# Weights of a matmul with batch norm: a pair of blocks first, two single blocks behind

## The chip, the cores and the metric

The kernel runs on one core of a Trainium2 chip. The metric is the device time of one execution in microseconds (us), the median of three runs. The core has five engines with their own instruction streams: PE (TensorE, matmuls; its weight loads are listed as PEld), DVE (VectorE), ACT (ScalarE), POOL (GpSimd) and SP (SyncE, which here issues stores and DMA transposes). Sixteen DMA engines move the data.

## The reference

```python
batch, m, k, n = 16, 512, 1024, 768

def reference(x, weight, gamma, beta, eps):
    y = np.matmul(x, weight)
    mean = np.mean(y, axis=(0, 1), keepdims=True)
    var = np.var(y, axis=(0, 1), keepdims=True)
    y_norm = (y - mean) / np.sqrt(var + eps)
    return (gamma * y_norm + beta).astype(np.float32)
```

The rows of all batches form one matrix of 8192 x 1024, multiplied by a 1024 x 768 weight matrix. Each of the 768 columns of the product is normalised over all its 8192 rows. All arrays are float32.

## The kernel before, in words

**Tiles.** The 8192 rows are cut into 16 chunks of 512 (`CH`). The first two chunks are loaded in halves of 256 rows (`QR`), the later ones whole. Every load converts float32 to bf16 on the way, and only POOL issues such loads. A load of x is four issues, one for each quarter of the 1024 elements of k, each into 32 partitions (L386 to L394). DVE then turns the chunk (STREAM_TRANSPOSE, L403 to L422) so that k lies on the partitions; for chunk 0 each half is turned in two pieces, of two blocks of k each. The turned chunk is the tile `xT_sb`.

**Weights.** k is cut into four blocks (`JW` = 4), numbered by `jw`; one block of w covers 256 elements of k, all 768 columns. `load_w(jw, jw1)` (L378) loads the blocks from jw up to jw1, again with four issues, each into 32 partitions. `w_ready` holds the load task by its first block; `waits` (L592) lets a matmul unit wait for all loads of w whose first block is at most its own last block.

**Loads in order.** The list `order` (L426 to L431) writes the order of the loads by hand: `("x", 0)` is the first half of chunk 0, which is called x0 here, then x1 (its second half), x2 and x3 (the halves of chunk 1); `("w", a, b)` is the load of blocks a to b - 1. Before, this is x0, block 0, x1, block 1, blocks 2 and 3 together, x2, x3, then whole chunks.

**Matmuls.** The first 256 columns (two column tiles, `GA`) are computed with rows on the partitions (`rows_unit`, L598, matmuls at L493); the other 512 columns, four column tiles, with columns on the partitions (`col_unit`, L610, matmuls at L558). `part(q0, q1, jws)` (L757) does for the halves q0 up to q1 of chunk 0 all products with the blocks in `jws`. The order before (L763 to L771) is: first half with block 0; a filler; second half with block 0; both halves with block 1; both halves with blocks 2 and 3 together. Then, from L822 on, the later chunks follow: rows, then columns for the first chunks; the other columns are computed after the loads are over.

**Warm-up and filler.** TensorE begins with `WAKE` = 8 matmuls of zeros in float32 (L574; each is two instructions) and `SMALL` = 22 small ones in bf16 (L577). The filler is the same float32 matmul, `FILL` times.

**Statistics.** When a row unit is done, ACT squares it (L642), DVE adds the rows (L645), POOL or DVE adds the squares (L649), and ACT keeps a bf16 copy (L655). When a column unit is done, DVE takes its statistics (L694) and ACT keeps a copy (L698). Eight PSUM banks hold the results until then.

**Planner.** Nothing is issued in the order of the code. Each piece of work becomes a `Task` with a priority (a due time), the engines it can run on, an assumed duration and what it depends on. `arrange` (L122) plays the schedule through with these durations and writes a fixed order of instructions for every engine. `clock[0]` (L580) adds up the assumed durations of TensorE's work and gives the due times of what follows. The class `Wires` assumes eight loads in flight for each queue (`LANES`).

Of the kernel before, what the change touches and what calls it, by code (L numbers as in the profile page):

```python
# [227 lines left out]
def kernel(  # L228
# [20 lines left out]
    NT = N // P  # L249
# [6 lines left out]
    JW = KQ // 64  # L256
    PIECES = ((0,QR),(QR,QR))
    WAKE = 8
    FILL = 2
    SMALL = 22  # L260
    TOUCH = 1
    EARLY = 4
    SHORT = 2
    GA = 2
# [26 lines left out]
    def seq(bi):  # L291

        ins = bi.ins
        prev = last.get(ins.engine)
        if prev is not None:
            tc.add_manual_dep(
                ins, prev,
                mybir.DependencyInfo(mybir.DependencyClass.NoSync, mybir.DependencyReason.DATA),
                reason="order",
            )  # L300
        last[ins.engine] = ins.name
        return bi
# [48 lines left out]
    def task(prio, engines, emit, deps=(), lock=False, **kw):  # L351
        t = Task(prio, engines, emit, deps, **kw)
        t.lock = lock
        tasks.append(t)
        return t

    def dve(occ):
        return {"DVE": (occ, occ + 0.09)}

    def act(occ):  # L360
        return {"ACT": (occ, occ + 0.11)}
# [14 lines left out]
    w_ready, x_ready, x_slot, plain, last_loads = {}, {}, {}, {}, []  # L376

    def load_w(jw, jw1):  # L378
        def emit(eng):
            rows = weight.rearrange("(i jw c e) n -> i c jw (e n)", i=4, jw=JW, e=2)  # L380
            dst = w_sb.rearrange("p jw e n -> p jw (e n)")
            for i in range(4):
                seq(nc.gpsimd.dma_start(dst[32 * i:32 * i + 32, jw:jw1], rows[i, :, jw:jw1]))
        return emit

    def load_x(m0, rows, slot):  # L386
        def emit(eng):
            x_bf = piece(slot).bitcast(bf16).rearrange("p (t k) -> p t k", k=KQ)
            slot.tile = x_bf
            src = x_flat[m0:m0 + rows].rearrange("(t r) k -> r t k", r=32)  # L390
            for i in range(4):
                bi = seq(nc.gpsimd.dma_start(x_bf[32 * i:32 * i + 32], src[:, :, KQ * i:KQ * (i + 1)]))  # L392
            slot.loader.ins = bi.ins
        return emit  # L394
# [28 lines left out]

    for c in range(C):
        x_slot[c] = Slot(xts)
    order = [("x", 0), ("w", 0, 1)] + [("x", 1), ("w", 1, 2), ("w", 2, 4)]  # L426
    order += [("x", q) for q in range(2, SHORT * QPC)] + [("c", c) for c in range(SHORT, C - 1)]
    at = M - CH
    for rows in (CH-P,P):
# [2 lines left out]
    t = 1.0  # L432
    affine = None
    for kind, n, *n1 in order:
        if kind == "w":
            took = 4 * 192 * 4 * (n1[0] - n) / 4 * PER_KB * 1.024
            w_ready[n] = task(t, {"POOL": (2.0, 2.0)}, load_w(n, *n1), dma=took)
            w_ready[n].count = 4
            t += 2.1 * (n1[0] - n)
            if n1[0] == JW:  # L440
                idt = task(t, {"POOL": (0.6, 0.6)}, lambda eng: make_identity(nc, ident))
                task(t, act(0.25), lambda eng: seq(nc.scalar.copy(ident32, ident)), [idt])
            continue
        rows = n1[0] if kind == "p" else QR if kind == "x" else CH
        m0 = n if kind == "p" else n * rows
        if m0 == M // 2:
            affine = task(t, {"SP": (5.0, 7.0)}, load_affine, [x_ready[m0 // CH - 3, 0, JW]])
        slot = Slot(rings, rows // 32 * KQ // 2)
        load = task(
            t, {"POOL": (2.68 * rows / CH, 2.68 * rows / CH)}, load_x(m0, rows, slot), dma=rows * K * 4 / 1024 * PER_KB * 1.024,  # L450
            takes=[slot])
        load.count = 4
        slot.loader = load
        last_loads.append(load)
        t += 2.7 * rows / QR
        for i in range(rows // QR):
            c, q = divmod(m0 // QR + i, QPC)
            for j0, j1 in ((0, JW // 2), (JW // 2, JW)) if m0 < CH else ((0, JW),):
                new = q == 0 and j0 == 0
                x_ready[c, q, j1] = task(  # L460
                    -1000 + t, dve((2.2 if c in SINGLE else 1.16) * (j1 - j0) / JW + 0.02),
                    turn_x(slot, x_slot[c], m0, i * QR // 32, j0, j1, new), [load],
                    uses=[slot] if new else [slot, x_slot[c]], takes=[x_slot[c]] if new else [])
                if not new:
                    x_ready[c, q, j1].deps.append(x_ready[c, 0, JW // 2 if m0 < CH else JW])
            x_ready.setdefault((c, q, JW // 2), x_ready[c, q, JW])
        if rows % QR:
            t0 = rows // QR * QR // 32
            m1 = m0 + 32 * t0
            c, q = divmod(m1 // QR, QPC)  # L470
            x_ready["tile", m1 // P] = task(
                -1000 + t, dve(0.63), turn_x(slot, x_slot[c], m0, t0, 0, JW, False, P),
                [load, x_ready[c, 0, JW]], uses=[slot, x_slot[c]])
            x_ready[c, q, JW] = x_ready[c, q, JW // 2] = x_ready["tile", m1 // P]
# [95 lines left out]
    def wake(count, slot):  # L570
        def emit(eng):
            idle_ps = psum.tile([P, CH], f32, tag="b")
            for _ in range(count):
                seq(nc.tensor.matmul(idle_ps, idle_sb[:, 0:P], idle_sb, start=True, stop=True))  # L574
            small = idle_sb[:, 0:P // 2].bitcast(bf16)
            for _ in range(SMALL if count == WAKE else 0):
                seq(nc.tensor.matmul(idle_ps[:, 0:P], small, small, start=True, stop=True))  # L577
        return emit
# [5 lines left out]
    def pe_task(occ, emit, deps, key=None, **kw):  # L584
        t = task(clock[0], pe(occ), emit, deps, **kw)
        t.after = begun.get(key)
        begun[key] = t if key else None
        emit.task = t
        clock[0] += occ
        return t  # L590

    def waits(jws, c, q0, q1):  # L592
        return [w_ready[w] for w in w_ready if w <= jws[-1]] + [
            x_ready[c, q, JW // 2 if jws[-1] < JW // 2 else JW] for q in range(q0, q1)]
# [3 lines left out]
    def rows_unit(c, ts, jws=range(JW)):  # L598
        key = "row", c, ts[0]
        slot = bank_of.setdefault(key, None) or Slot(banks)  # L600
        bank_of[key] = slot
        kw = {"takes": [slot], "uses": [x_slot[c]]} if jws[0] == 0 else {"uses": [slot, x_slot[c]]}
        h = ts[0] * P // QR
        t = pe_task(0.873 * len(ts) * len(jws) / JW, mm_rows(c, ts, list(jws), slot),
                    waits(jws, c, h, h + 1), key, **kw)
        if jws[-1] == JW - 1:
            rows_stats(c, ts, slot, t)
        return t

    def col_unit(nt, c, jws, q0=0, q1=QPC):  # L610
        slot = bank_of.setdefault((nt, c), None) or Slot(banks)
        bank_of[nt, c] = slot
        first = jws[0] == 0 and q0 == 0
        xs = [plain[c][0][jw] for jw in jws] if c in plain else [x_slot[c]]
        kw = {"takes": [slot], "uses": xs} if first else {"uses": [slot] + xs}
        t = pe_task((1.728 if c in plain or c in SINGLE else 1.808) * len(jws) / JW * (q1 - q0) / QPC,
                    mm(nt, c, list(jws), slot, q0, q1),
                    waits(jws, c, q0, q1) + ([plain[c][1][jw] for jw in jws] if c in plain else []), (nt, c), **kw)
        if q1 - q0 == QPC:
            t.hosts = 4  # L620
        if jws[-1] == JW - 1 and q1 == QPC:
            col_stats(nt, c, slot, t)
        return t
# [133 lines left out]
    def part(q0, q1, jws):  # L757
        for h in range(q0, q1):
            rows_unit(0, [2 * h, 2 * h + 1], jws)
        for nt in range(GA, NT):  # L760
            col_unit(nt, 0, jws, q0, q1)

    part(0, 1, [0])  # L763
    fill_slot = Slot(banks)
    pe_task(0.87 * FILL, wake(FILL, fill_slot), [w_ready[0]], takes=[fill_slot])
    part(1, 2, [0])
    part(0, 2, [1])
    for h in range(2):
        rows_unit(0, [2 * h, 2 * h + 1], [2, 3])
    for nt in range(GA, NT):  # L770
        col_unit(nt, 0, [2, 3])  # L771

    halves = [range(JW // 2), range(JW // 2, JW)]
    merges = []
# [455 lines left out]
    nt = NT - 1  # L1230
# [40 lines left out]
    for c, r0, rows in ends:  # L1271
        due = E + 2.0 + 0.6 * c
        n = max(rows // CH, 1)
# [30 lines left out]
    order = arrange(tasks, turns)  # L1304
# [39 lines left out]
```

## Time and profile before

| what | value |
|---|---|
| runs | 208.77, 208.78, 208.35 us; median 208.77 |
| span of the profiled execution | 206.5 us |
| loads of x by POOL: issues of 256 KB | 52, median 8.8 us from issue to landing |
| loads of w by POOL: issues of 96 KB (one block) | 8, median 5.1 us to landing |
| loads of w by POOL: issues of 192 KB (two blocks) | 4, median 5.9 us to landing |
| turns of x0 and x1 on DVE, each in two pieces | begin at 8.49 and 13.45 us, 1.31 and 1.30 us |
| turns of x2 and x3 on DVE | begin at 22.65 and 25.71 us |
| four issues of x0 on POOL | from 1.29 us, 2.44 us |
| four issues of block 0 of w on POOL | from 3.73 us, 1.99 us |
| one issue of x1 on POOL | 5.84 us, and the next at 6.76 us |

The span is the time from the first to the last record of one profiled execution; the measured time of a run is longer, since it holds what lies around the span. A KB in the sizes is counted as the data is written to SBUF, in bf16. L12 is line 12 of the kernel. The granted clock is the share of TensorE's full clock that it was given. A line of the timeline merges neighbouring instructions of one kind; its length is that of the group, so neighbouring groups of matmuls, which are pipelined, overlap a little.

### The profile page before, as it was taken

Reading aid. Unit: us, or ns where it says so; the run is one execution under the profiler, and the core shown is the slowest. Engines: PE = TensorE matmul, PEld = TensorE weight load, DVE = VectorE, ACT = ScalarE, POOL = GpSimd, SP = SyncE. Lnnn points to the kernel's source line nnn. Section 1 sums busy time; section 2 is a strip of 40 time slices with the busy share of each in tenths; the row PEclk is TensorE's granted clock in tenths of the full one; section 3 lists DMA queues with packets and bytes.
Section 4 is the critical chain, followed back from the end, with each engine's and each line's share of the span. In section 5 each row is a group of like instructions: output and inputs, shape, how many; then the busy total and the mean of one; then the engine's idle time right before and its main releaser. Section 6 shows DMA issues by size and latency. Waiting matters only on the chain.

```text
span 206.5 us, 3506 instructions
## 1 busy us (share of the span) xinstructions
PE 191.4 (93%) x1211; PEld 116.3 (56%) x1226; DVE 156.3 (76%) x238; ACT 139.8 (68%) x248; POOL 132.0 (64%) x148
## 2 busy tenths in 40 slices
PE   7998999999999999999999999999999999996900
PEld 3465564747488888777875444444444445553600
DVE  4220779999999999968989998977999648947900
ACT  2000560369989999998978767997376776866950
POOL 7877964877488999999304999599954440440000
PEclk9999999999999999999999999999999999999995
DMA  5999999999999999999676898999999999999898
GB/s 55 169 168 193 192 196 196 196 198 197 190 193 197 197 197 195 196 197 195 110 120 199 311 339 307 267 350 307 315 317 245 291 325 308 274 341 347 254 347 243
DMA packets 98497, 48.73 MB, mean 236 GB/s; under 512 B 24240, under 2 KB 97968, under 8 KB 98480
## 3 DMA queue, kind: packets, MB, share of 16 engines
q0 software_dynamic: 34688, 18.36, 65.1%
q1 hardware_dynamic: 63792, 30.16, 52.8%
q8 instruction: 9, 0.15, 0.3%
q14 instruction: 8, 0.07, 0.1%
HBM read 36.71 MB, written 25.17 MB: 300 GB/s over the span
## 4 chain that ended last, share of the span: by engine, by line
PE 82%; DMA 8%; ACT 3%; issue 1%; POOL 1%; DVE 1%; ACTq 0%; POOLq 0%
PE y_ps L558 51%; PE y_ps L493 23%; DMA ring<-in_x_dram 5%; PE y_ps L798 4%; ACT o_sb L1293 3%; DMA w_sb<-in_weight_dram 3%; PE o_ps L1028 2%; PE a_ps L887 1%; POOL ring L392 1%; PE y_ps L736 1%; PE o_ps L1058 0%; ACTq L1339 0%; PE tot_ps L855 0%; DVE fin L743 0%; ACT y_sb L746 0%
## 5 line engine op out<-in xcount | busy, mean ns | idle before, releaser
L558 PEld LDWEIGHTS <-w_sb 128*128 128x128 bf16 x512 | 49.7, 97 | 57.4
L558 PE MATMUL y_ps<-x_pl,w_sb 128*128 128x512 bf16 x256 | 60.5, 379 | 0.3
L392 POOL DMA_DIRECT2D ring<-in_x_dram x76 | 47.5, 630 | 13.0 <-DVE xT_sb L414 5.0
L558 PE MATMUL y_ps<-xT_sb,w_sb 128*128 128x512 bf16 (+1 forms) x241 | 55.1, 376 | 0.4
L493 PE MATMUL y_ps<-w_sb,xT_sb 128*128 128x256 bf16 x448 | 50.7, 273 | 0.6 <-DMA w_sb<-in_weight_dram 0.6
L493 PEld LDWEIGHTS <-xT_sb 128*128 128x128 bf16 x448 | 43.6, 98 | 8.3 <-issue 1.7
L421 DVE STREAM_TRANSPOSE xT_sb<-ring 128x1024 f32<-128x1024 f32 (+1 forms) x29 | 31.2, 1111 | 12.4 <-DMA ring<-in_x_dram 12.2
L694 DVE BATCH_NORM_STATS2 stats<-y_ps 128x6 f32<-128x512 f32 x46 | 30.9, 687 | 12.7 <-PE y_ps L558 12.5
L698 ACT CAST y_sb<-y_ps 128x512 bf16<-128x512 f32 x51 | 29.4, 590 | 14.5 <-DVE stats L694 12.4
L926 POOL TENSOR_TENSOR ring<-ring,sum 128x1024 f32<-128x1024 f32 (+1 forms) x11 | 23.7, 2193 | 14.6 <-DVE ring L921 14.5
L649 POOL TENSOR_TENSOR sum<-sum,sq_sb 128x512 f32<-128x512 f32 x21 | 26.9, 1281 | 3.2 <-ACT sq_sb L642 2.1
L642 ACT ACTIVATE sq_sb<-y_ps 128x512 f32<-128x512 f32 x28 | 16.3, 607 | 18.0 <-PE y_ps L493 17.1
L645 DVE TENSOR_TENSOR sum<-y_ps,sum 128x512 f32<-128x512 f32 x28 | 18.9, 675 | 9.1 <-ACT sq_sb L642 7.8
L530 ACT COPY x_pl<-xT_sb 128x1024 bf16<-128x1024 bf16 x24 | 24.4, 1052 | 1.7 <-DVE xT_sb L421 1.7
L655 ACT CAST y_sb<-y_ps 128x512 bf16<-128x512 f32 x28 | 16.0, 599 | 7.8 <-DVE sum L645 7.6
L530 POOL COPY x_pl<-xT_sb 128x1024 bf16<-128x1024 bf16 x15 | 16.1, 1108 | 8.0 <-DVE x_pl L530 5.2
L921 DVE TENSOR_TENSOR ring<-y_sb,a_ps 128x1024 f32<-128x1024 bf16 (+1 forms) x16 | 16.7, 1080 | 0.3 <-DMA out_dram<-ring 0.3
L1139 POOL TENSOR_TENSOR ring<-ring,sum 128x1024 f32<-128x1024 f32 x4 | 9.6, 2412 | 11.0 <-DVE ring L1135 11.0
L1193 ACT CAST ring<-ring 128x1024 f32<-128x1024 bf16 x15 | 15.7, 1049 | 1.0 <-DMA ring<-y_sb 1.0
L1028 PE MATMUL o_ps<-ident,y_sb 128*128 128x128 bf16 x104 | 14.2, 221 | 2.2 <-DVE y_sb L1280 2.0
L414 DVE STREAM_TRANSPOSE xT_sb<-ring 128x2048 bf16<-128x2048 bf16 x6 | 13.5, 2289 | 0.2 <-DMA ring<-in_x_dram 0.2
L574 PE MATMUL idle_ps<-idle_sb 128*128 128x512 f32 x20 | 11.2, 717 | 1.5 <-DVE idle_sb L314 1.5
(97 smaller groups left out, 155.0 us busy)
## 6 DMA issues: line engine op xcount, KB each, us to landing
out_dram<-ring SPq DMA_DIRECT2D x38, 512.0 KB, 3.7
ring<-in_x_dram POOLq DMA_DIRECT2D x52, 256.0 KB, 8.8
out_dram<-o_sb SPq DMA_DIRECT2D x6, 512.0 KB, 4.9
ring<-in_x_dram POOLq DMA_DIRECT2D x16, 128.0 KB, 5.3
out_dram<-ring SPq DMA_DIRECT2D x4, 256.0 KB, 3.0
w_sb<-in_weight_dram POOLq DMA_DIRECT2D x8, 96.0 KB, 5.1
w_sb<-in_weight_dram POOLq DMA_DIRECT2D x4, 192.0 KB, 5.9
ring<-in_x_dram POOLq DMA_DIRECT2D x4, 192.0 KB, 8.1
```

The lines of the kernel that those rows point to most:

```text
L392: bi = seq(nc.gpsimd.dma_start(x_bf[32 * i:32 * i + 32], src[:, :, KQ * i:KQ * (i + 1)]))
L421: seq(nc.vector.transpose(dst, src[:, :, jw0:jw1]))
L493: seq(nc.tensor.matmul(y_ps[:, s], x_of(c, jw, e, t * P, (t + 1) * P), w_sb[:, jw, e, 0:NA], start=(s == 0 and jw == 0 and e == 0), stop=( ...
L530: seq(nc.scalar.copy(dst, pairs) if eng == "ACT" else ENG[eng].tensor_copy(dst, pairs))
L558: seq(nc.tensor.matmul(y_ps, w_sb[:, jw, e, nt * P:(nt + 1) * P], moving(c, jw, e, q0 * QR, q1 * QR, parted), start=(jw == 0 and e == 0 an ...
L645: seq(nc.vector.tensor_add(sum1, slot.tile[:, 0:n], sum1))
L649: seq(ENG[eng].tensor_add(acc, acc, state["sq"][:, 0:n]))
L694: seq(nc.vector.bn_stats(dst, slot.tile))
L698: seq(nc.scalar.copy(y(nt, c), slot.tile))
L921: seq(nc.vector.tensor_mul(slot.o, y_row[c].y[:, s0:s1], aff[0][:, None, :].to_broadcast([P, n, NA])))
L926: seq(ENG[eng].tensor_add(slot.o, slot.o, row[:, None, :].to_broadcast([P, n, NA])))
L1028: seq(nc.tensor.transpose(dst, src, ident))
```

## The change

```diff
-    FILL = 2
-    SMALL = 22
+    FILL = 1
+    SMALL = 34
...
-    order = [("x", 0), ("w", 0, 1)] + [("x", 1), ("w", 1, 2), ("w", 2, 4)]
+    order = [("x", 0), ("w", 0, 2), ("x", 1), ("w", 2, 3), ("w", 3, 4)]
...
-            w_ready[n] = task(t, {"POOL": (2.0, 2.0)}, load_w(n, *n1), dma=took)
+            w_ready[n] = task(t, {"POOL": (2.14, 2.14)}, load_w(n, *n1), dma=took)
...
-    part(0, 1, [0])
+    part(0, 1, [0, 1])
     fill_slot = Slot(banks)
     pe_task(0.87 * FILL, wake(FILL, fill_slot), [w_ready[0]], takes=[fill_slot])
-    part(1, 2, [0])
-    part(0, 2, [1])
-    for h in range(2):
-        rows_unit(0, [2 * h, 2 * h + 1], [2, 3])
-    for nt in range(GA, NT):
-        col_unit(nt, 0, [2, 3])
+    part(1, 2, [0, 1])
+    part(0, 2, [2])
+    part(0, 2, [3])
```

The loads become: x0, blocks 0 and 1 of w together, x1, block 2, block 3, x2, x3. TensorE does the first half of chunk 0 with blocks 0 and 1 (half of k), one filler matmul, the second half with blocks 0 and 1, then both halves with block 2 (a quarter of k), and both halves with block 3. Twelve more small matmuls stand at the end of the warm-up. The planner assumes 2.14 us of POOL's time for a load of w instead of 2.0. The number of issues stays: four double and eight single ones for w.

## The prediction

> **What bounds the kernel now.** I read the page's busy times and the chain that ended last, then the waits of TensorE, then the first 30 us engine by engine, then the bytes moved in each 2 us. The page first.
>
> ```profile
> span 206.5 us, 3506 instructions
> PE 191.4 (93%) x1211; PEld 116.3 (56%) x1226; DVE 156.3 (76%) x238; ACT 139.8 (68%) x248; POOL 132.0 (64%) x148
> PE 82%; DMA 8%; ACT 3%; issue 1%; POOL 1%; DVE 1%; ACTq 0%; POOLq 0%
> ```
>
> TensorE bounds it: 82% of the chain. The waits of TensorE, whole list (total, times, longest):
>
> ```profile
> PE o_ps L1028 <- DVE y_sb L1280: 2.0, 1, 2.0
> PE idle_ps L574 <- DVE idle_sb L314: 1.5, 1, 1.5
> PE y_ps L493 <- DMA w_sb<-in_weight_dram: 0.6, 1, 0.6
> ```
>
> One is at the start, one at the very end (190.9 us), and one, 0.6 us, in chunk 0. From 20 to 189 us TensorE waits for nothing listed, so what TensorE gains or loses before 29 us should reach the end one for one. The places that matter, from the timeline (start, length, engine, line, what; in brackets the idle time before and what ended it):
>
> ```profile
> 10.67 1.39 PE L577 MATMUL idle_ps<-idle_sb 128*128 128x128 bf16 x22
> 11.89 0.60 PE L493 MATMUL y_ps<-w_sb,xT_sb 128*128 128x256 bf16 x4
> 13.24 1.88 PE L574 MATMUL idle_ps<-idle_sb 128*128 128x512 f32 x4
> 19.74 1.91 PE L493 MATMUL y_ps<-w_sb,xT_sb 128*128 128x256 bf16 x16 [0.60 <-DMA w_sb<-in_weight_dram]
> 25.10 3.83 PE L493 MATMUL y_ps<-w_sb,xT_sb 128*128 128x256 bf16 x32
> 25.71 1.25 DVE L421 STREAM_TRANSPOSE xT_sb<-ring 128x1024 f32<-128x1024 f32 x1 [0.64 <-DMA ring<-in_x_dram]
> 27.01 1.64 PEld L493 LDWEIGHTS <-xT_sb 128*128 128x128 bf16 x16 [0.28 <-DVE xT_sb L421]
> ```
>
> Chunk 0 runs from 11.89 to 25.10. The first half of chunk 1 follows at 25.10, and its second half at 27.01 is loaded into TensorE only when VectorE has turned it: it lands at about 25.6, is turned from 25.71 to 26.96, and TensorE's weight load waits 0.28 us for it. So **a second limit lies right under the first**: even if chunk 0 ended much earlier, TensorE would stand before this half until 26.96. The stretches of 2 us (busy us of each engine, then granted clock, DMA share, GB/s):
>
> ```profile
> 2.00:4.00 2.00, 2.00 (x3) 0.66 (x2) 1.04 (x4) 0.22 (x2) 2.00 (x5) 1.00 0.60 63
> 4.00:6.00 2.00, 2.00 (x4) 0.74 (x3) 0.00 (x0) 0.00 (x0) 2.00 (x6) 1.00 1.15 130
> 6.00:8.00 2.00, 2.00 (x6) 0.90 (x5) 0.00 (x0) 0.30 (x1) 1.34 (x4) 1.00 1.14 166
> 8.00:10.00 2.00, 2.00 (x6) 0.95 (x5) 1.31 (x2) 0.00 (x0) 1.86 (x4) 1.00 1.19 188
> 10.00:12.00 2.00, 2.00 (x25) 1.42 (x24) 0.00 (x0) 0.00 (x0) 1.86 (x5) 1.00 1.35 177
> 12.00:14.00 2.00, 2.00 (x16) 1.46 (x13) 0.55 (x1) 0.00 (x0) 1.35 (x3) 1.00 1.07 157
> 14.00:16.00 2.00, 2.00 (x13) 1.20 (x12) 0.75 (x2) 0.00 (x0) 1.46 (x4) 1.00 1.04 177
> 16.00:18.00 2.00, 1.94 (x16) 1.42 (x15) 0.00 (x0) 0.00 (x0) 1.56 (x4) 1.00 1.08 207
> 18.00:20.00 2.00, 1.40 (x9) 0.55 (x7) 0.00 (x0) 0.00 (x0) 1.25 (x3) 1.00 1.28 182
> ```
>
> The clock is 1.00 throughout. Adding GB/s x 2 us gives the bytes moved: 0.39 MB by 6 us, 0.72 by 8, 1.09 by 10, 1.45 by 12, 1.76 by 14, 2.12 by 16, 2.53 by 18, 2.89 by 20; the next stretches read 193 and 197, so 3.28 by 22 and 3.67 by 24. The loads are 0.524 MB for a half chunk of x and 0.393 MB for a block of w as written to SBUF. In order, x0+w0+x1 are 1.44 MB, reached at 12.0 us; its last issue lands at about 13.32. All of w is 2.62 MB, reached at 18.5; it lands at about 19.6. x3 (chunk 1's second half) ends at 3.67 MB, reached at 24.0; it lands at 25.6. So **a load lands 1.1 to 1.7 us after its bytes are through; I use 1.35**. GpSimd issues every load itself, and its waits show that the ninth load waits for the first to land (5.84 us, after x0's first, issued at 1.29 and landing 4.5 us later), the next for the second, and so on: eight are in flight.
>
> **The change, part by part.** The sum is made on the profiled execution (span 206.5 us); the runs' median is 208.77, so 2.3 us lie outside the span, which I leave as they are.
>
> *Warm-up, 22 to 34 small matmuls.* They go from 10.67 to 11.89, 0.0555 us each; 12 more are 0.67 us and end at 12.56.
>
> *First w as a pair.* The four issues start at 3.73 as before; the four double ones of before took 0.54 each against 0.50, so GpSimd ends 0.1 us later, before the lane wait at 5.84 that paces x1: no cost. x0 and the pair are 1.31 MB, reached at 11.2, landing at 12.57. Bounds: 11.3 (last issue 5.34, and the doubles of before landed 5.9 us after issue) and 12.9 (lag 1.7). Up to 12.56 the warm-up covers it. I take 12.6, 0.7 us later than 11.89.
>
> *Chunk 0.* A half of one block is 1.35 us (11.89 to 13.24), a whole one 2.7 (two of them from 19.74 to 25.10 are 5.4). The first half of the pair is 2.70: 12.6 to 15.3. The filler falls from two calls to one; two took 1.72 (13.24 to 14.96), so 0.86: to 16.2. x1 ends at 1.835 MB, reached at 14.4, lands at 15.8, and VectorE's first piece (0.65, half of the 1.30 at 13.45) is done at 16.5. TensorE waits 0.3 us there. Second half: 16.5 to 19.2. Block 2 lands at 17.9 (2.23 MB at 16.5) and block 3 at 19.6 to 19.9: both are there in time, so the 0.6 us wait goes. Block 2 runs to 21.9, block 3 to 24.6. Chunk 0 ends **0.5 us earlier** than 25.10. Block 1 is now done in halves, 16 column matmuls of 256 for 8 of 512: 1.82 us (8 took 0.91, from 12.33 to 13.24) against 1.73, and the 0.09 is within the 2.70. Banks: six for chunk 0, two for chunk 1's rows, as before.
>
> *Statistics of chunk 0.* The row sums become due at 22.4 instead of 20.8, and the four column sums (0.68 each on VectorE) come within 2 us instead of 4. VectorE has 3.3 us from 22.4 to 25.7 for one turn of x (1.24) and three row operations (0.69, 0.68, 0.65): it just fits, at nothing, as long as no column sum is put before the turn of x3.
>
> *Loads behind.* The number of issues is unchanged, but eight in flight now hold less: singles stand where the doubles stood, just ahead of x2 and x3. By "landing of the eighth before, plus 0.25" and 0.6 us per x issue: block 2 is issued at 9.6, 10.7, 11.7, 12.8; block 3 at 13.6, 14.4, 15.2, 16.0; x2 from 16.6 (before 14.67); x3's last at **20.75 against 19.89**. In between the transfers in hand (issued over 1.3 us ago and not yet moved) shrink to about 0.2 MB from 17 to 21 us; in the run before they were that few near 12 us, where the row reads 157 GB/s. What x3 loses has two ends: nothing, if bytes set its landing (25.6 as before), and 0.86 us, if its last issue again takes 5.7 us to land, which is what x issues of 17 to 20 us took. x1's issues with as little in hand took 4.7 to 4.8, so neither end is excluded; I take the middle, **0.43 us late**.
>
> A rule of the Trainium skill stands on the other side. "DMA: Bandwidth & Descriptors", section "Anatomy of one DMA — SWDGE (gpsimd) path", fits a GpSimd load as about 2.0 us plus its bytes over 436 GB/s. For x3's last issue that is an estimate of some 2.6 us, landing at 23.4: TensorE would then never wait for it, and the sum would be 0.5 us faster, 208.3. The trace disagrees for such loads (5.7 us), because others are ahead in the queue.
>
> *Sum.* TensorE reaches chunk 1 at 24.6, ends its first half (1.75) at 26.4, and waits for x3: 26.96 + 0.43 = 27.4, against 27.01. The 0.5 us won in chunk 0 is lost in that wait, and **0.4 us is added: 209.2**. Behind it wait chunk 1's columns, and for them chunk 2's rows at 36.0; those need VectorE's turns of 31.09 to 35.59, 0.4 us of slack. They move along with the statistics.
>
> **Rivals.** *The other side, not slower:* the pair puts more in flight early, so the dip at 12 to 14 us (157 against about 190 around it: 0.066 MB, 0.35 us) is filled and no new one opens. x3 then lands 0.35 early, TensorE starts its second half at 26.6, and the time is 208.4, at best 208.2, where chunk 0's end decides (26.4). It decides as soon as x3 lands before 25.6. For: chunk 0's shorter end is sure. Against: 0.86 us of later issue.
>
> *Bytes alone set the landing:* second half at 26.96, no idle elsewhere, 208.7. For: 195 GB/s without gaps from 20 us on. Against: the thin queue before.
>
> *VectorE becomes the bound:* the planner's list puts one more sum (0.68) ahead of the turn of x3, which cannot give way. Then 27.4 + 0.5 to 0.68: 209.7 to 209.9. For: VectorE's 3.3 us fill the gap exactly, and the planner's due times move by 0.87 with the shorter filler, so that its whole list is made anew. Against: in the run before it waited 0.64 us idle for x3.
>
> **How the numbers follow.** Late x3: 0.43, own range 208.8 to 209.7 (0 to 0.86 late), a little over half of it slower by more than 0.2% (0.42 us, about what a measurement of this kernel tells from no change). VectorE: 0.20, slower. Bytes alone: 0.12, no change. More in flight: 0.25, of which 0.18 is beyond the bound. Faster 0.18; same 0.07 + 0.12 + 0.19 = 0.38; slower 0.24 + 0.20 = 0.44. The range, 208.2 to 210.1, goes from the best end of the faster case to VectorE's worst with a queue lag 0.2 more.
>
> **What would show it.** Right: TensorE's first real matmul near 12.6; no wait for w in chunk 0; a wait of 0.5 to 1 us of the row matmuls for the turn of x3 near 27; x3's last issue near 20.7; the remaining chain shifted as a whole. Wrong: x3 turned before 26.9; new waits between 30 and 189 us; a first matmul later than 13.2, which would move every step of chunk 0.

## The result, and the profile after

The changed kernel takes 210.4 us (median of five runs, 210.31 to 210.92) against 208.4 us of the kernel before in the same series; the ratio is 1.0115, with a 95% interval of 1.0091 to 1.014. That is slower by 2.0 us between the medians and by 2.4 us by the ratio, and the median lies 0.3 us beyond the upper end of the predicted range. The profiled execution has a span of 208.9 us, 2.4 more than the 206.5 before. Medians and ratios differ by some tenths of a us in the runs below too; where it matters, both are given.

The page of the changed kernel begins so:

```profile
span 208.9 us, 3557 instructions
PE 192.0 (92%) x1244; PEld 118.6 (57%) x1244; DVE 155.4 (74%) x237; ACT 140.0 (67%) x248; POOL 133.4 (64%) x149
...
PE 53%; POOL 14%; DMA 13%; DVE 6%; issue 6%; ACT 3%; ACTq 0%; DVEq 0%; POOLq 0%
```

TensorE is still the busiest engine, but it is only 53% of the chain that ended last, where it was 82% before; loads of x and their issues on GpSimd (DMA and POOL) have taken its place there. TensorE also holds more instructions: 12 more small warm-up matmuls, 8 more column matmuls (16 of 256 columns for 8 of 512) and 2 fewer in the filler make 18, and as many weight loads (1244 for 1226), so 36 instructions. Its waits, all of them:

```profile
PE o_ps L1025 <- DVE y_sb L1277: 2.0, 1, 2.0
PE idle_ps L574 <- DVE idle_sb L314: 1.5, 1, 1.5
PE y_ps L493 <- DVE xT_sb L421: 1.1, 2, 0.9
PE y_ps L493 <- ACT y_sb L698: 0.3, 1, 0.3
PE y_ps L493 <- DMA w_sb<-in_weight_dram: 0.3, 1, 0.3
```

The 0.6 us wait for w inside chunk 0 is gone; the 0.3 us left stands ahead of the first matmul. In its place are two waits for turned x (0.9 us at 25.7 us, 0.2 at 81.5) and one for ScalarE at 46.2. The timeline of TensorE and VectorE where chunk 0 ends (lines are three lower than before behind the change):

```profile
12.23 1.03 PE L493 MATMUL y_ps<-w_sb,xT_sb 128*128 128x256 bf16 x8 [0.26 <-DMA w_sb<-in_weight_dram]
23.82 1.91 PE L493 MATMUL y_ps<-w_sb,xT_sb 128*128 128x256 bf16 x16
25.32 1.25 DVE L421 STREAM_TRANSPOSE xT_sb<-ring 128x1024 f32<-128x1024 f32 x1
26.63 1.92 PE L493 MATMUL y_ps<-w_sb,xT_sb 128*128 128x256 bf16 x16 [0.90 <-DVE xT_sb L421]
```

Chunk 0 ends 1.3 us earlier (23.82 against 25.10), and chunk 1's second half begins 0.38 us earlier (26.63 against 27.01). So in this execution the start was won, and the loss lies behind it. Two stretches hold it. Chunk 3's rows begin 0.09 us later than before (46.49 against 46.40), the columns that follow the long row stretch 0.49 later (85.23 against 84.74), and TensorE's last long group 0.66 later (185.81 against 185.15): 1.04 us are lost between 27 and 106 us. And from there to the end of the span another 1.7 us are lost, though all the lists of work there are the same. The DMA rate from 195 to 209 us, in 40 slices of 0.35 us, first of the kernel before, then of the changed one, each with the queue lines that differ:

```profile
GB/s 340 345 348 351 344 348 347 345 348 348 345 350 347 342 348 351 345 340 348 351 348 351 340 345 348 351 344 348 193 7 0 0 0 0 0 23 0 0 0 0
...
q14 instruction: 1, 0.01, 0.2%
```

```profile
GB/s 344 345 174 332 388 328 328 318 332 335 345 302 350 347 350 344 345 348 350 347 342 347 350 348 344 347 347 348 348 344 350 70 20 22 22 22 3 0 0 0
...
q8 instruction: 1, 0.02, 0.6%
```

Before, the stores end all at once (the lone 23 behind them is the 8 KB transfer on q14). After, the rate drops to 174 once, at 195.7 to 196.1, and at the end some 22 GB/s go on alone for 1.7 us. 348 over 16 is 21.8: that is **one DMA engine of sixteen, 1.7 us behind the others**. On queue q8, which carries only such transfers, stands one transfer of 16 KB of instructions that the kernel before does not have there. In the trace's packets it begins at 196.63 us; the last store has landed on fifteen engines by 206.36 and on the sixteenth at 208.01. Over the whole run the kernel before has nine such transfers, the last at 179.5 us, and the changed one ten.

So the 2.4 us between the two profiles are 0.66 us of TensorE's lag, 1.48 us of the late engine (1.75 us behind the median engine, where it was 0.27) and 0.25 us more in the stores of the other engines: these land 0.68 us later than before at 196.2 us and 0.85 to 0.91 later from 197.9 on, behind the slice at 174 GB/s. What made that slice is not known.

### The profile page after: what moved, and what is told of

Its sections match the earlier page's. It is cut to its first block, busy times and chain, and to the rows that moved or that the text cites. A ratio compares the mean times of both kernels' runs of the same rounds, so it can differ in the third digit from the quotient of the medians.

```text
span 208.9 us, 3557 instructions
## 1 busy us (share of the span) xinstructions
PE 192.0 (92%) x1244; PEld 118.6 (57%) x1244; DVE 155.4 (74%) x237; ACT 140.0 (67%) x248; POOL 133.4 (64%) x149
## 4 chain that ended last, share of the span: by engine, by line
PE 53%; POOL 14%; DMA 13%; DVE 6%; issue 6%; ACT 3%; ACTq 0%; DVEq 0%; POOLq 0%
PE y_ps L558 39%; DMA ring<-in_x_dram 10%; POOL ring L392 9%; PE y_ps L493 5%; PE y_ps L795 3%; DMA w_sb<-in_weight_dram 3%; POOL sum L649 3%; ACT o_sb L1290 2%; PE o_ps L1025 2%; DVE xT_sb L421 2%; POOL w_sb L383 2%; DVE xT_sb L414 1%; DVE stats L694 1%; PE a_ps L884 1%; PE y_ps L736 1%
## 5 line engine op out<-in xcount | busy, mean ns | idle before, releaser
L558 PEld LDWEIGHTS <-w_sb 128*128 128x128 bf16 x520 | 50.5, 97 | 56.6
L558 PE MATMUL y_ps<-x_pl,w_sb 128*128 128x512 bf16 x264 | 61.3, 379 | 0.0
L558 PE MATMUL y_ps<-xT_sb,w_sb 128*128 128x512 bf16 (+1 forms) x256 | 55.9, 370 | 0.0
L649 POOL TENSOR_TENSOR sum<-sum,sq_sb 128x512 f32<-128x512 f32 x22 | 28.2, 1281 | 2.7 <-ACT sq_sb L642 2.0
L574 PE MATMUL idle_ps<-idle_sb 128*128 128x512 f32 x18 | 9.6, 686 | 1.5 <-DVE idle_sb L314 1.5
```

What stands on the lines that cost most here:

```text
L558: seq(nc.tensor.matmul(y_ps, w_sb[:, jw, e, nt * P:(nt + 1) * P], moving(c, jw, e, q0 * QR, q1 * QR, parted), start=(jw == 0 and e == 0 an ...
L649: seq(ENG[eng].tensor_add(acc, acc, state["sq"][:, 0:n]))
```

## The experiments

Theory F: the tenth instruction transfer delays one DMA engine and so the end. Theory L: the planner's new list, the order of work that it makes for every engine, costs TensorE the 1.04 us. When L fell, theory Q took its place (single blocks behind the pair let the queue of loads run thin), against P (the pieces of chunk 0 or the pair in front).

**a_small18: fewer TensorE instructions in the changed kernel**

```diff
-    SMALL = 34
+    SMALL = 18
```

> The changed kernel with 18 small warm-up matmuls instead of 34: 32 TensorE instructions fewer, nothing else. Theory F (code fetch): in the profile of the changed kernel a tenth 16 KB instruction transfer begins at 196.6 us, when TensorE has 19 instructions left, and from then on one of the 16 DMA engines ends every store 1.75 us after the others; the kernel before has nine such transfers, the last at 179.5 us. With 32 instructions fewer the tenth is not reached: the last store ends on all engines within 0.4 us and the time falls by 1.3 to 1.6 us, from 210.4 to 208.9. The shorter warm-up ends 0.9 us earlier but the first pair of w lands at 12.2 us as before, so nothing is lost there. Rival L (the planner's list alone costs the 2 us): no change, 210.4.

Measured: 209.27 us, ratio to the kernel before 1.0046 (1.0028 to 1.0065), against 1.0115 of the changed kernel. By the ratios 1.4 us of the 2.4 are gone, as F expected; by the medians 1.1, and the median stands 0.4 us above the expected one. There are nine instruction transfers, and the same view of the end:

```profile
GB/s 345 348 341 347 348 350 345 347 347 347 347 347 350 347 347 342 350 348 350 340 347 350 350 342 347 347 348 350 345 347 170 0 0 0 0 0 0 23 0 0
```

No engine is left behind. What remains is TensorE's own lag, 0.68 us at its last long group (185.83). Here x3's half is turned from 26.00, and chunk 1's second half begins at 27.30, 0.29 late:

```profile
24.07 1.92 PE L493 MATMUL y_ps<-w_sb,xT_sb 128*128 128x256 bf16 x16
27.30 0.94 PE L493 MATMUL y_ps<-w_sb,xT_sb 128*128 128x256 bf16 x7 [1.31 <-DVE xT_sb L421]
```

**b_more_pe: more TensorE instructions in the kernel before**

```diff
-    WAKE = 8
+    WAKE = 6
-    SMALL = 22
+    SMALL = 53
```

> The kernel before with two float32 warm-up matmuls fewer and 31 small ones more: the warm-up takes as long as before (1.72 us out, 1.72 us in), the planner's lists of all other engines are the same, and TensorE has some 54 instructions more. Theory F: a tenth 16 KB instruction transfer falls into the last stores, one DMA engine ends about 1.7 us late, and the time rises by 1.3 to 1.7 us, from 208.4 to about 209.9. Rival L: no change, 208.4.

Measured: 209.51 us, ratio 1.0074 (1.0046 to 1.0102): slower by 1.5 us by the ratio, by 1.1 between the medians. TensorE stands where it stood (185.05 against 185.15), and the end has the lone engine again, with the tenth transfer at 196.94 us:

```profile
GB/s 340 344 335 342 347 380 326 323 334 339 350 345 347 344 348 350 350 337 350 350 348 342 348 345 350 350 345 345 107 22 20 22 18 0 0 0 0 0 0 23
...
q8 instruction: 1, 0.02, 0.4%
```

Taken away from one kernel and put into the other, the transfer carries 1.4 and 1.5 us by the ratios, 1.1 both times by the medians. Among all nine profiles of this case the last store has a late engine (by 1.49 to 1.75 us) in just the three with a tenth transfer, and none by more than 0.27 in the six others (table below). F is shown. The Trainium skill ("Runtime: NRT & Kernel Launch", section "Instruction fetch mechanics") says that an engine's code is refilled in blocks of 16 KiB, 256 instructions, and that crossing a boundary is mostly hidden. The blocks agree with the trace: each transfer has 16 KB, and one comes every 248 to 256 TensorE records on average (176 to 322 between two of them). That the cost is hidden holds for the ninth: in the kernel before, the store of 181 us ended on one engine 1.84 us after the median, and this lag was down to 0.25 us by 195.8, after the gap between the stores at 192 us. The tenth came with no gap behind it. No run here singles out what the first eight cost.

**a_listB and b_listA: the planner's lists exchanged**

```diff
-    order = arrange(tasks, turns)
+    order = follow(tasks, turns)
```

Here `follow` takes a fixed list of task, engine and time, that which the planner made for the other kernel; the tasks of both correspond one to one.

> The changed kernel (its loads, its pieces of chunk 0, its warm-up), but every engine follows the list that the planner made for the kernel before, task by task. Theory L in part (the list costs what TensorE loses between 27 and 106 us: it was 0.38 us ahead at chunk 1's second half and 0.66 us behind at 185 us, 1.04 us in all): TensorE stays ahead, and the time falls by about 1.0 us, from 210.4 to 209.4; the tenth instruction transfer stays, as the number of instructions does. Rival (the loss between 27 and 106 us comes from when the loads land, not from the list): within 0.3 us of 210.4.

> The kernel before (its loads, its pieces of chunk 0, its warm-up), but every engine follows the list that the planner made for the changed kernel. Theory L in part: TensorE loses about 1.0 us between 30 and 106 us, and the time rises from 208.4 to 209.4, with no late DMA engine at the end. Rival (loads, not the list): within 0.3 us of 208.4.

Measured: b_listA 208.35 us, ratio 1.0004 (0.9986 to 1.0022); a_listB 212.26 us, ratio 1.0178 (1.014 to 1.0217). The kernel before loses nothing with the changed kernel's list, and the changed kernel gains nothing from the old list but loses 1.3 us more by the ratios, 1.9 by the medians. **Theory L fell.** Why the old list hurts the changed kernel can be read from VectorE's timeline of a_listB:

```profile
22.51 0.69 DVE L645 TENSOR_TENSOR sum<-y_ps,sum 128x512 f32<-128x512 f32 x1 [6.17 <-ACT sq_sb L642]
23.11 2.43 DVE L649 TENSOR_TENSOR sum<-sum,sq_sb 128x512 f32<-128x512 f32 x1
25.46 1.23 DVE L421 STREAM_TRANSPOSE xT_sb<-ring 128x1024 f32<-128x1024 f32 x1
```

It puts a row sum and a sum of squares of chunk 0 ahead of the turn of x2, and these now come later: x2 is turned at 25.46 instead of 22.14, and TensorE waits 2.7 us. The new list turns x2 first. Not all of the 2.7 us is the order, though: the sum of squares took 2.43 us here, where the usual one takes 0.68, for a reason that no run shows.

What the three profiles with the changed loads so far have in common is the loads themselves. The stretches of 2 us of the changed kernel (last number: GB/s):

```profile
14.00:16.00 2.00, 2.00 (x15) 1.24 (x13) 1.06 (x2) 0.00 (x0) 1.60 (x4) 1.00 1.10 206
16.00:18.00 2.00, 2.00 (x20) 1.74 (x18) 0.25 (x1) 0.00 (x0) 2.00 (x5) 1.00 1.12 192
18.00:20.00 2.00, 2.00 (x17) 1.45 (x15) 0.00 (x0) 0.00 (x0) 2.00 (x4) 1.00 1.20 117
20.00:22.00 2.00, 2.00 (x14) 1.25 (x13) 0.00 (x0) 0.22 (x1) 1.81 (x4) 1.00 1.41 184
22.00:24.00 2.00, 2.00 (x12) 0.93 (x11) 1.82 (x2) 0.87 (x3) 1.97 (x3) 1.00 1.29 169
24.00:26.00 2.00, 1.73 (x16) 1.31 (x14) 1.93 (x3) 1.77 (x4) 2.00 (x4) 1.00 1.27 162
```

Up to 16 us the pair is ahead: 2.30 MB of loads have moved, against 2.12 before. Then the rate falls to 117 from 18 to 20 us (182 before), again to 169 and 162 from 22 to 26 (197 and 187 before), and by 28 us 4.32 MB have moved, against 4.43. From there on the loads run at 195 GB/s without a break until about 95 us, so the 0.1 MB, 0.5 us, is not made up: 14.41 against 14.51 MB at 80 us.

**b_singles: the kernel before with blocks 2 and 3 singly**

```diff
-    order = [("x", 0), ("w", 0, 1)] + [("x", 1), ("w", 1, 2), ("w", 2, 4)]
+    order = [("x", 0), ("w", 0, 1)] + [("x", 1), ("w", 1, 2), ("w", 2, 3), ("w", 3, 4)]
```

> The kernel before with blocks 2 and 3 of w loaded one after the other instead of together; the lists of TensorE, VectorE, ScalarE and SyncE are the same, GpSimd has four load issues more. Theory Q (thin queue): eight issues are in flight at most, and with single blocks in them the queue ahead of x2 and x3 runs dry; in the three profiles with single blocks there, the loads moved 89 to 125 GB/s in the stretch from 18 to 19 us and 1.27 to 1.34 MB from 16 to 24 us, in the three with a double block 161 to 181 GB/s and 1.48 to 1.54 MB. The same hole must open here, x is turned late, TensorE waits some 0.5 to 1 us near 27 us and the time rises by 0.5 to 1.0 us, to about 209.1. Rival P (the pieces of chunk 0 or the pair in front cause the loss): no change, 208.4.

Measured: 210.03 us against 207.95, ratio 1.0081 (1.0053 to 1.0109). The loss is larger than expected, 1.7 us by the ratio and 2.1 between the medians, and the eleven runs lie wide apart, 208.69 to 211.27. The profile is of a run of 209.15 and shows only the smaller loss; what the runs of 210 us and more lose besides is not known. No piece of chunk 0 and no entry in the lists of TensorE, VectorE, ScalarE and SyncE has changed, and the hole opens (view as above):

```profile
16.00:18.00 2.00, 2.00 (x17) 1.47 (x16) 0.00 (x0) 0.00 (x0) 1.83 (x4) 1.00 0.98 171
18.00:20.00 2.00, 1.71 (x10) 0.75 (x9) 0.00 (x0) 0.00 (x0) 1.57 (x4) 1.00 0.90 112
20.00:22.00 2.00, 2.00 (x17) 1.50 (x16) 0.68 (x2) 1.03 (x2) 1.31 (x3) 1.00 1.43 190
```

TensorE waits 0.39 us near 27 us, less than expected, and 0.44 again at 81.7. The profile puts this second wait to a square on ScalarE, but the weight load at the same place waits 0.72 us for turned x, and VectorE, which had waited 1.31 us for x until 64.9, has worked almost without a pause since. At its last long group TensorE is 0.88 us behind (186.03). So the second wait at 81 us, where x just keeps pace with the row matmuls, collects what the loads lost at 18 us. A code transfer is not what makes the hole: TensorE's first falls at 17.6 us in the changed kernel, but at 23.7 here, behind the hole.

**b_loadsA: the kernel before with the changed kernel's loads**

```diff
-    order = [("x", 0), ("w", 0, 1)] + [("x", 1), ("w", 1, 2), ("w", 2, 4)]
+    order = [("x", 0), ("w", 0, 2), ("x", 1), ("w", 2, 3), ("w", 3, 4)]
...
-            w_ready[n] = task(t, {"POOL": (2.0, 2.0)}, load_w(n, *n1), dma=took)
+            w_ready[n] = task(t, {"POOL": (2.14, 2.14)}, load_w(n, *n1), dma=took)
```

> The kernel before with the loads of the changed kernel (pair first, then x1 and two single blocks), but its own pieces of chunk 0, its own warm-up and so its own number of TensorE instructions. Theory Q: the hole at 18 us opens, about 0.2 MB less by 24 us, TensorE is 0.5 to 0.7 us behind at 185 us, no tenth instruction transfer, 209.0. Rival P (the pieces): within 0.3 us of 208.4.

Measured: 209.29 us, ratio 1.006 (1.0038 to 1.0081), 1.3 us slower where 0.6 had been expected. 3.54 MB have moved by 24 us against 3.66 before; TensorE waits 1.34 us for x3's half at 26.6, and is 0.93 behind at its last long group (186.08). All of the 0.93 is lost at x3 here, and there is no second wait at 81 us. There are nine instruction transfers and no lone engine. The planner made a new list for this run too (TensorE's pieces stand in another order than before), but a new list alone cost nothing in b_listA, and b_singles has the loss with the lists unchanged. So the loads make this part of the loss, and not the four more issues of b_singles either, since this run has as many as the kernel before; P fell.

**a_two_pairs: the changed kernel with both pairs whole**

```diff
-    SMALL = 34
+    SMALL = 18
...
-    order = [("x", 0), ("w", 0, 2), ("x", 1), ("w", 2, 3), ("w", 3, 4)]
+    order = [("x", 0), ("w", 0, 2), ("x", 1), ("w", 2, 4)]
...
-    part(0, 2, [2])
-    part(0, 2, [3])
+    for h in range(2):
+        rows_unit(0, [2 * h, 2 * h + 1], [2, 3])
+    for nt in range(GA, NT):
+        col_unit(nt, 0, [2, 3])
```

> The changed kernel with blocks 2 and 3 loaded together behind x1 and multiplied together (half and half of k), and 18 small warm-up matmuls. Theory Q with theory F: no hole at 18 us, no tenth instruction transfer, so both losses go and TensorE keeps what it wins in chunk 0: 0.3 to 0.5 us faster than the kernel before, 208.0, and 1.2 us faster than the run with 18 small matmuls alone. Rival P: no better than that run, 209.3.

Measured: 207.65 us against 207.95, ratio 0.998 (0.9962 to 0.9998): a little faster than the kernel before, the fastest here. The stretch of the hole, and TensorE's first real matmul:

```profile
16.00:18.00 2.00, 2.00 (x16) 1.44 (x15) 0.92 (x2) 0.00 (x0) 1.33 (x3) 1.00 1.09 202
18.00:20.00 2.00, 1.93 (x18) 1.46 (x16) 0.00 (x0) 0.00 (x0) 1.22 (x3) 1.00 1.42 192
20.00:22.00 2.00, 2.00 (x16) 1.38 (x15) 0.92 (x2) 1.27 (x3) 1.88 (x4) 1.00 1.44 193
```

```profile
12.91 1.03 PE L493 MATMUL y_ps<-w_sb,xT_sb 128*128 128x256 bf16 x8 [1.66 <-DMA w_sb<-in_weight_dram]
24.74 3.65 PE L493 MATMUL y_ps<-w_sb,xT_sb 128*128 128x256 bf16 x32
```

The hole is closed, x2's first issue comes at 13.72 us instead of 15.58, and all of chunk 1 follows at 24.74 without a wait. Though TensorE idles 1.66 us before its first matmul, it is 0.54 us ahead at its last long group (184.61 against 185.15). A dip from 22 to 26 us is here too (171 and 178), so that second dip is not the single blocks' doing; the hole from 18 to 20 us is.

All runs side by side (ratio to the kernel before; start of TensorE's last long group; how long after the median of the sixteen engines the last store ends on the last one, in the profile):

| run | ratio | last long group, us | last engine, us |
|---|---|---|---|
| before | 1 | 185.15 | 0.27 |
| changed kernel | 1.0115 | 185.81 | 1.75 |
| a_small18 | 1.0046 | 185.83 | 0.12 |
| b_more_pe | 1.0074 | 185.05 | 1.59 |
| a_listB | 1.0178 | 187.21 | 1.49 |
| b_listA | 1.0004 | 184.90 | 0.10 |
| b_singles | 1.0081 | 186.03 | 0.15 |
| b_loadsA | 1.0060 | 186.08 | 0.23 |
| a_two_pairs | 0.9980 | 184.61 | 0.21 |

## Why the prediction was right or wrong

The forecast's side was right (slower), its size was not: 0.4 us above the median of 208.77 that it was given, where 2.0 to 2.4 us were measured against the kernel before in the same series, outside the range. The right side is partly luck: in the changed kernel's own profile the loss that was forecast, a late x3, is not there, since x3 landed 0.39 us earlier than before (25.20 against 25.59) and its matmuls began 0.38 us early. The time was lost at two places to which the forecast gave no price.

- *Warm-up, and chunk 0's narrow matmuls.* Priced by their time alone: 0.67 us for the warm-up, 0.09 for the narrow columns. That was right as far as it went (first real matmul predicted at 12.6, measured 12.23). **The step that failed is here:** the 36 added instructions were given no price as instructions. They brought a tenth code transfer among the last stores, which the exchanged runs price at 1.4 and 1.5 us by the ratios (1.1 by the medians). The forecast held that what TensorE gains or loses before 29 us should reach the end one for one; it had a fixed tail behind TensorE, and the tail is not fixed.
- *The pair.* Right: no cost at its issue, no wait for w inside chunk 0.
- *Chunk 0's end.* Predicted at 24.6, measured at 23.82 in the changed kernel and 24.07 in a_small18: the gain there was under-rated by 0.5 to 0.8 us. In a_small18 all of it was lost in the wait for x3, as predicted; in the changed kernel 0.90 of 1.28.
- *Loads behind.* That the queue runs thin behind 17 us was right, that x3 is issued later was not. Its last issue came at 19.57, not at 20.75, since w landed faster; that is 0.32 us before the 19.89 of the kernel before. Yet the rate fell to 117, where 157 had been the worst row behind 8 us to go by. The forecast's other term, 5.7 us from x3's last issue to its landing, measured 5.6 in the changed kernel and 6.5, 5.9 and 6.9 in a_small18, b_singles and b_loadsA. x3's turn, predicted 0.43 late, was 0.39 early in the changed kernel's profile, and 0.26 to 0.93 late in a_small18, b_singles and b_loadsA.
- *Sum.* Here a second step failed: what the loads lost was counted at x3 only. It stays in the stream of loads, which has no slack until some 95 us, and where TensorE has lost less than that at x3, it meets the rest at 81 to 87 us. The term of 0.4 us measured 0.66 us in the changed kernel's profile, 0.68 in a_small18, 0.88 in b_singles and 0.93 in b_loadsA. The 0.31 us that TensorE waited for ScalarE at 46.2 probably cost nothing in the end, as the wait for x at 81.5 would have been longer by as much; no run tests this.
- *Rivals.* "More in flight" was right up to 16 us and wrong behind. "VectorE becomes the bound" was missed by a hair: the list puts one more sum between the turns of x2 and x3, and VectorE goes from the turn of x2 to that of x3 without a pause, but x3 is turned 0.12 us after it landed, as in the kernel before, where VectorE had waited for it. The old list would have made VectorE the bound (a_listB). The fit of the Trainium skill ("DMA: Bandwidth & Descriptors", section "Anatomy of one DMA — SWDGE (gpsimd) path"), 2.0 us plus the bytes, did not hold for x3 behind other loads: 19.57 to 25.20 us, so 5.6 us.
- *Signs.* As forecast: the first matmul near 12.6, no wait for w in chunk 0, a wait of 0.5 to 1 us for x3 (0.90). Two signs of being wrong came as well: x3 was turned before 26.9 us (by 26.57), and new waits stood between 30 and 189 us.
- *A reading.* x0's first issue landed 3.5 us after it was issued (1.29 to 4.76); the 4.5 us of the forecast is the median of its four issues. That eight loads are in flight still follows from the later issues, which go out 0.3 us behind the landing of the load eight places before.

What stays open: whether the thin queue comes of eight smaller issues in flight or of x2's issue coming too short a time before the last of w is through; all runs here change both. The second has a plain source. x2's first issue goes out 0.28 to 0.30 us behind the landing of the load eight places before it in each of these profiles: block 1's first (14.39 us) in the kernel before, block 2's first in the changed kernel (15.29) and in b_singles (15.07), x1's first in a_two_pairs (13.44).

## What to carry to other kernels

Where loads without slack follow a change, what they lose stays lost until their stream ends, so sum it there and not at the first tile that waits. Before adding instructions, even free ones, count where the engine's next block of code will be fetched: a fetch among the last stores was on the path here. Here the split of the last transfers ahead of a steady stream (b_singles, ratio 1.0081) was dearer than what the single block at the very front cost (the kernel before against a_two_pairs, ratio 0.998, where the pieces and the warm-up differ too).

## What the runs showed of the hardware

- A 16 KB transfer of instructions took 0.9 to 1.4 us itself. Behind the ninth and tenth of them, which fall into the stream of stores, the stores of these profiles ended on one of the sixteen DMA engines 0.7 to 2.1 us after the median engine. The engine made up little while stores were queued on all engines (1.84 us at 182.9, 1.71 at 193.5 in the kernel before), and caught up only in a gap (0.25 at 195.8). A store is complete only when its last engine is.
- Behind the last of w the loads took some time to come back to their full rate: in the changed kernel x2's first issue went out at 15.58 us and landed at 19.98, the last of w landed at 18.65, and the rows of 2 us read 117, 184, 169 and 162 GB/s from 18 to 26 us, and 195 behind.
